# Ten feed-forward tiles of the first MLP go through the down product as seven block products

## The chip, the cores and the metric

The kernel runs on one core of one Trainium2 chip. The metric is the device time of one execution in microseconds (us). Its engines work side by side, each in its own program order, and wait for one another by semaphores: TensorE (PE, matrix products), VectorE (DVE), ScalarE (ACT), GpSimd (POOL), and SyncE (SP), which here issues DMA transfers.

## The reference

A trunk of two pre-norm layers over 512 tokens of width 1024: layer 0 has grouped-query and latent attention, layer 1 neighbourhood attention. After each attention stands the same kind of MLP, and the end is an RMSNorm. All is float32.

```python
def rmsnorm(x, g):
    return x * lax.rsqrt(jnp.mean(x * x, axis=-1, keepdims=True) + EPS) * g

def sq_relu_mlp(h, w_up, w_down):          # w_up 1024 x 4096, w_down 4096 x 1024
    u = jax.nn.relu(h @ w_up)
    return (u * u) @ w_down

# in each of the two layers:
x = x + attention(rmsnorm(x, g_attn))
x = x + sq_relu_mlp(rmsnorm(x, g_ffn), w_up, w_down)
```

## The kernel before

**Number format.** A float32 matrix is kept as two parts of PE's reduced format fp32r: `hi`, a rounded copy made by ACT, and `lo`, the rest, made by DVE as a subtraction. A product is three matmuls, hi by hi, hi by lo and lo by hi. Weights arrive by DMA as `raw`, and become `whi` (ACT L212, or L306 for block products) and `wlo` (DVE L202, L307). They are loaded five chunks ahead of their use, and converted two ahead.

**Slots.** Thirty slots of [128, 1024] float32 hold what lives through the MLP: the normalised tokens, the hidden tiles `U` and raw weight chunks where a slot is free (otherwise one of four `raw` buffers).

**Plain product.** `product` takes for each of four output tiles (four PSUM banks) and for each tile of the summed dimension three matmuls of 512 columns (L496, L497, L498).

**Seven block products.** Class `Seven` takes two output tiles and two k-tiles (a k-pair) as a 2 x 2 block matrix, and the 512 tokens as two halves of 256, and forms the product from seven block products instead of eight. For that it needs sums and differences of blocks on both sides. On the weights' side `seven_chunk` loads 256 KB and makes three subtractions on POOL (L300, L301, L302) for each k-pair. On the token side `sums` makes three subtractions on POOL (L335 to L337), and `split` makes hi (ACT L358) and lo (DVE L359). `run` is then 21 matmuls of 256 columns for each k-pair (L383, L384, L385), and the end of a pair of tiles puts the seven results together: one copy on ACT (L391) and four additions on DVE (L392 to L395).

**The MLP.** The hidden width of 4096 is 32 tiles, taken in four stages of 6, 10, 8 and 8 tiles (`SIZES`). A stage makes its hidden tiles by the up product (relu and square on ACT, L1131 and L1132, and hi and lo, ACT L822 and DVE L819), and then adds their down product to the residual stream `hT` (DVE L1223). The first six tiles are plain (`plain`): there the tokens aren't normalised yet, and each result is scaled by the tokens' `rb` (DVE L1116, ACT L1118). The other 26 come in 13 pairs by `Seven` from normalised tokens `x7`, over four k-pairs (1024 / 256). All down products are plain: a stage of n tiles is 8 output tiles by n k-tiles by 3 matmuls, so 24 n matmuls of 512 columns. While the first down product runs, `later` is called after each of its steps, and issues at the steps (0, 2), (0, 10), (0, 18) and (1, 4) a whole split of one k-pair of x7 (four hi and four lo) at once.

**What sets the order.** The program is written as generators. A scheduler puts the instructions of each engine in an order of its own, by estimated costs; a yielded number is the estimate for a step of PE. `tc.keep_in_program_order` pins an instruction to the place on its engine where the code wrote it.

**After the MLP.** Behind the first MLP stands layer 1's value projection `valuesC`, which takes hT times the norm's weights (ACT L502, DVE L503) as its tokens, and the sum of squares `acc` (ACT L510, DVE L512) for the norm, which PE adds up over the partitions at L517. The last MLP ends the program, with a function of its own; its down product has the lines L1565 to L1567, and the transposes L1579 to token order, which ACT copies at L1580.

Of the kernel before, what the change touches and what calls it, by code (L numbers as in the profile page):

```python
# [16 lines left out]
S = 512  # L17
D = 1024
P = 128
# [16 lines left out]
def encoder_kernel(ctx: ExitStack, tc: tile.TileContext, ins, out, dbg=None):  # L36
# [253 lines left out]

    SEVEN = [(0, 0), (2, 2), (4, 5), (3, 3), (5, 4), (6, 1), (1, 6)]

    def seven_chunk(w, k0, c0):


        slot = Slot(F32) if len(free) > 1 else None
# [3 lines left out]
        POOL.tensor_tensor(r[:, 6], r[:, 0], r[:, 1], op=ALU.subtract)  # L300
        POOL.tensor_tensor(r[:, 4:6], r[:, 2:3].to_broadcast([P, 2, P]), r[:, 0:7:6], op=ALU.add)  # L301
        POOL.tensor_tensor(r[:, 7], r[:, 3], r[:, 5], op=ALU.subtract)  # L302
        yield
        hi = wp.tile([P, 1024], F32R, tag="whi", name=nm("whi"))
        lo = wp.tile([P, 1024], F32R, tag="wlo", name=nm("wlo"))
        ACT.activation(hi[:, 0:896], raw[:, 128:1024], AF.Copy)  # L306
        DVE.tensor_tensor(lo[:, 0:896], raw[:, 128:1024], f32(hi[:, 0:896]), op=ALU.subtract)  # L307
        if slot:
            slot.free()
        yield hi, lo, []  # L310

    class Seven:
# [6 lines left out]
            self.np = nk // 2  # L319

        def number(self, kp, b):
            return 3 * kp + b if b < 3 else 3 * self.np + 4 * kp + b - 3
# [6 lines left out]
        def sums(self, kp, fill_x):  # L329
            raw, t = Slot(F32), Slot(F32)  # L330
# [5 lines left out]
            POOL.tensor_tensor(t_[:, 2], r[:, 2], t_[:, 0], op=ALU.subtract)  # L336
            POOL.tensor_tensor(t_[:, 3], r[:, 3], t_[:, 2], op=ALU.subtract)  # L337

        def split(self, kp):
            for b in range(7):  # L340
                i = self.number(kp, b) // 2
                if i not in self.slots:
                    self.slots[i] = Slot()
            raw, t = self.raw.pop(kp)
            r, t_ = (s_.t.rearrange("p (b n) -> p b n", n=256) for s_ in (raw, t))
            b = 0
            while b < 7:
                q = self.number(kp, b)
                n = 2 if b in (3, 5) or (b < 2 and q % 2 == 0) else 1
                s_ = r[:, 1 + b : 1 + b + n] if b < 3 else t_[:, b - 3 : b - 3 + n]  # L350
                if n == 1:
# [7 lines left out]
                DVE.tensor_tensor(lo, s_, f32(hi), op=ALU.subtract)  # L359
                b += n  # L360
            raw.free()
            t.free()

# [1 line left out]
            for s_ in self.slots.values():  # L365
                s_.free()

        def plan(self, w, c0):
            return [plan(w, 2 * kp, c0, make=seven_chunk) for kp in range(self.np)]

        def run(self, ids, evac):

            bk = group(4)
            half = lambda b, z: b[:, 256 * z : 256 * z + 256]

            dst = [(bk[0], 0), (bk[1], 0), (bk[1], 1), (bk[2], 0), (bk[2], 1), (bk[3], 0), (bk[3], 1)]
            for kp in range(self.np):
                hi, lo = weights(ids[kp])
                for (a, b), (bank_, z) in zip(SEVEN, dst):
                    x = self.at(kp, b)  # L380
                    wh, wl = (y[:, P * a : P * a + P] for y in (hi, lo))
                    o = half(bank_, z)
                    PE.matmul(o, wh, x[:, 0], start=kp == 0 and z == 0, stop=False, skip_group_check=True)  # L383
                    PE.matmul(o, wh, x[:, 1], start=False, stop=False, skip_group_check=True)  # L384
# [6 lines left out]
            ACT.activation(r[:, 3], half(bk[0], 0), AF.Copy)  # L391
            DVE.tensor_tensor(r[:, 1:3], r[:, 3:4].to_broadcast([P, 2, 256]), two(bk[1]), op=ALU.add)  # L392
            DVE.tensor_tensor(r[:, 0:4:3], r[:, 2:3].to_broadcast([P, 2, 256]), two(bk[2]), op=ALU.add)
            DVE.tensor_tensor(r[:, 2], r[:, 3], half(bk[2], 0), op=ALU.add)
            DVE.tensor_tensor(r[:, 0:4:3], r[:, 0:4:3], two(bk[3]), op=ALU.add)  # L395
            evac(w_)
            w_.free()

    flip = [0]

# [693 lines left out]

    SIZES = (6, 10, 8, 8)

    def first_product(l):

# [7 lines left out]
        U = []  # L1108
        rb = keep([P, S], F32, "rb")
        state = dict(c=SIZES[0], ids=None, plain=False)  # L1110
        x7 = Seven(KD)

        def ev(j, b):
# [13 lines left out]
        def fill_x(k, dst):  # L1127
            DVE.scalar_tensor_tensor(dst, hT[:, k, :], gffn(l, k), rb, op0=ALU.mult, op1=ALU.mult)

        def pair_evac(w_):  # L1130
            ACT.activation(w_.t, w_.t, AF.Relu)  # L1131
            ACT.activation(w_.t, w_.t, AF.Square)  # L1132
            first, second = Slot(), Slot()
            split(w_.t[:, S:], first.pair())
            split(w_.t[:, 0:S], second.pair())
            U.extend((first, second))

        def plain():
            four = product(w, 0, xp, tiles(0, 512), ev, lambda n: [mmb(), mmb(), mmb(), sbk()])
            two = product(w, 0, xp, tiles(512, 256), ev, lambda n: [sbk(), ob()], kstep=4)  # L1140
            for n, _ in enumerate(four):
                if n == (11 if l == 0 else 13):
                    norm()
                if n == 14:
                    x7.sums(0, fill_x)
                    x7.sums(1, fill_x)
            for n, _ in enumerate(two):
                if n == 4:
                    x7.sums(2, fill_x)
                if n == 6:  # L1150
                    x7.sums(3, fill_x)
# [12 lines left out]

        def stage(n):
            if not state["plain"]:
                plain()
            while len(U) < n:
                i = state["ids"]
                state["c"] += 2  # L1170
                if len(U) + 2 < n:
                    ahead()
                for _ in x7.run(i, pair_evac):
                    pass
            if state["c"] == 32:
                x7.free()
            got = list(U)
            U.clear()
            return got

        return stage, ahead, later
# [4 lines left out]
    def bias_rows():  # L1186
# [24 lines left out]
            s_.free()  # L1211
        yield

    def mlp(l):
        stage, ahead, later = first_product(l)
        bias = bias_rows()
        k0 = 0
        for z, n in enumerate(SIZES):
            U = stage(n)
            up = [s_.pair() for s_ in U]  # L1220

            def ev(m, b):
                DVE.tensor_tensor(hT[:, m, :], hT[:, m, :], b, op=ALU.add)  # L1223

            gens = [product(ins["ffn_w_down"][l], k0, up, tiles(512 * c, 512), lambda j, b, c=c: ev(4 * c + j, b))
                    for c in range(2)]
            k0 += n
            if k0 < 32:
                ahead()
            for c, gen in enumerate(gens):  # L1230
                for i, _ in enumerate(gen):
                    if z == 0:
                        later(c, i)
                    elif z == 1:
                        next(bias, None)
            for s_ in U:
                s_.free()

    mlp(0)

# [274 lines left out]
    def last_mlp(l):  # L1515
# [77 lines left out]
            return run  # L1593

        k0 = 0
        for n in SIZES:
            U = stage(n)
            if k0 == 0:
                H.extend(Slot(F32) for _ in range(4))
            last = k0 + n == 32  # L1600
# [66 lines left out]
```

## Time and profile before

| | |
|---|---|
| three runs, us | 1194.74, 1194.07, 1195.89 (median 1194.74) |
| the profiled execution, us | 1197.61 |
| its span, us | 1195.8 |
| mean granted PE clock | 0.997 |
| busy: PE, DVE, ACT, POOL, us | 1175.3, 797.0, 614.4, 421.1 |
| first MLP, down product of ten tiles | 386.53 to 442.49 |
| first MLP, last down product | 566.50 to 611.17 |

The span runs from the first to the last instruction; the execution's time holds 1.8 us more around it. PE is busy in 98% of the span, so the time is nearly that of PE's own instructions, and the places where PE waits are few.

### The profile page before, as it was taken

The numbers are of one execution on the slowest core, as the hardware profiler recorded it, in microseconds if no ns is written. First come the engines' busy times: TensorE is split into PE (matmuls) and PEld (weight loads), VectorE is DVE, ScalarE is ACT, GpSimd is POOL, SyncE is SP. The second block draws the span as 40 slices with busy tenths as digits, with TensorE's granted clock in tenths as the row PEclk, the third lists the DMA queues.
The fourth block names the chain that finished last, engine by engine and source line by source line (L and its number), as shares of the span: only waits on it lengthen the run. The fifth ranks groups of instructions, "written<-read, shape, count | busy, mean of one in ns | idle before, by whom it ended". The sixth has DMA issues, their size and how long they took to land.

```text
span 1195.8 us, 18740 instructions
## 1 busy us (share of the span) xinstructions
PE 1175.3 (98%) x6804; PEld 1010.0 (84%) x6804; DVE 797.0 (67%) x1411; ACT 614.4 (51%) x1037; POOL 421.1 (35%) x551
## 2 busy tenths in 40 slices
PE   9999999999999999999999999999999999999997
PEld 8677788887799889889888998988879988988985
DVE  4588988877867437547554676667984743664754
ACT  5577677764447226427433555545463641551653
POOL 3256252216564175341002232231454525434500
PEclk9999999999999999999999999999999999999999
DMA  7223314222522752430336574343342233333122
GB/s 253 64 56 91 86 53 133 71 62 80 176 70 69 228 178 71 133 98 27 105 88 176 129 180 128 114 113 98 115 132 79 63 123 97 98 116 115 54 89 71
DMA packets 105244, 127.96 MB, mean 107 GB/s; under 512 B 8787, under 2 KB 77312, under 8 KB 105152
## 3 DMA queue, kind: packets, MB, share of 16 engines
q1 hardware_dynamic: 102096, 119.30, 33.4%
q0 software_dynamic: 2304, 6.31, 2.2%
q10 hardware_dynamic: 752, 1.15, 0.4%
q8 instruction: 54, 0.88, 0.3%
q14 instruction: 38, 0.31, 0.1%
HBM read 104.32 MB, written 6.29 MB: 92 GB/s over the span
## 4 chain that ended last, share of the span: by engine, by line
PE 83%; DVE 7%; ACT 4%; POOL 3%; issue 2%; DMA 1%; POOLq 0%; DVEq 0%; ACTq 0%
PE mm L497 7%; PE mm L496 7%; PE mm L498 7%; PE mm L385 2%; PE mm L384 2%; PE mm L383 2%; PE s L986 2%; PE o L974 2%; PE s L496 2%; PE s L497 2%; PE s L498 2%; PE mm L1566 2%; PE mm L1565 2%; PE mm L1567 2%; PE t L961 2%
## 5 line engine op out<-in xcount | busy, mean ns | idle before, releaser
L202 DVE TENSOR_TENSOR wlo<-raw,whi 128x1024 fp32r<-128x1024 f32 (+2 forms) x135 | 159.7, 1186 | 142.4 <-ACT whi L212 131.4
L212 ACT ACTIVATE whi<-raw 128x1024 fp32r<-128x1024 f32 (+2 forms) x138 | 135.2, 981 | 167.8 <-PE o L497 38.0
L496 PE MATMUL mm<-a,whi 128*128 128x512 f32 x455 | 184.1, 406 | 0.2 <-DVE hT L920 0.2
L307 DVE TENSOR_TENSOR wlo<-a,whi 128x896 fp32r<-128x896 f32 x99 | 116.0, 1172 | 100.3 <-ACT whi L306 99.6
L497 PE MATMUL mm<-a,whi 128*128 128x512 f32 x455 | 181.0, 398 | 1.1 <-DVE a L819 1.0
L498 PE MATMUL mm<-a,wlo 128*128 128x512 f32 x455 | 180.7, 398 | 0.7 <-DVE wlo L202 0.7
L306 ACT ACTIVATE whi<-a 128x896 fp32r<-128x896 f32 x99 | 94.1, 951 | 142.4 <-PE o L384 26.9
L300 POOL TENSOR_TENSOR a<-a 128x128 f32<-128x128 f32 x99 | 61.8, 624 | 244.8 <-DMA a<-in_ffn_w_up_dram 207.0
L498 PEld LDWEIGHTS mm<-a,wlo 128*128 128x128 f32 x455 | 85.7, 189 | 22.1 <-issue 1.7
L497 PEld LDWEIGHTS mm<-a,whi 128*128 128x128 f32 x455 | 86.0, 189 | 20.0 <-issue 1.7
L496 PEld LDWEIGHTS mm<-a,whi 128*128 128x128 f32 x455 | 86.0, 189 | 19.1 <-issue 1.9
L301 POOL TENSOR_TENSOR a<-a 128x256 f32<-128x256 f32 x99 | 86.2, 871 | 7.8
L302 POOL TENSOR_TENSOR a<-a 128x128 f32<-128x128 f32 x99 | 80.3, 811 | 7.8
L385 PE MATMUL mm<-a,wlo 128*128 128x256 f32 x280 | 78.7, 281 | 0.7 <-DVE wlo L307 0.6
L384 PE MATMUL mm<-a,whi 128*128 128x256 f32 x280 | 78.6, 281 | 0.0
L383 PE MATMUL mm<-a,whi 128*128 128x256 f32 x280 | 78.5, 280 | 0.0
L994 POOL TENSOR_SCALAR p<-p,ti 128x512 f32<-128x512 f32 x64 | 46.0, 720 | 88.5 <-DVE ti L993 74.5
L1368 POOL TENSOR_SCALAR p<-p,ti 128x256 f32<-128x256 f32 x64 | 35.9, 571 | 105.5 <-DVE ti L1367 92.3
L384 PE MATMUL t<-a,whi 128*128 128x256 f32 x192 | 53.9, 281 | 0.0
L385 PE MATMUL t<-a,wlo 128*128 128x256 f32 x192 | 53.8, 280 | 0.0
L383 PE MATMUL t<-a,whi 128*128 128x256 f32 x192 | 53.8, 280 | 0.0
L385 PEld LDWEIGHTS mm<-a,wlo 128*128 128x128 f32 x280 | 52.7, 188 | 1.1 <-DVE wlo L307 1.1
(321 smaller groups left out, 3217.3 us busy)
## 6 DMA issues: line engine op xcount, KB each, us to landing
raw<-in_ffn_w_down_dram SPq DMA_DIRECT2D x64, 512.0 KB
a<-in_ffn_w_up_dram SPq DMA_DIRECT2D x99, 256.0 KB
raw<-in_od_w_qkv_dram SPq DMA_DIRECT2D x64, 128.0 KB
raw<-in_ffn_w_up_dram SPq DMA_DIRECT2D x12, 512.0 KB
raw<-in_ev_w_in_dram SPq DMA_DIRECT2D x12, 384.0 KB
a<-a SPq DMA_DIRECT2D x18, 256.0 KB
bias<-bx SPq DMA_DIRECT2D x16, 256.0 KB
raw<-in_od_w_qkv_dram SPq DMA_DIRECT2D x8, 512.0 KB
```

The lines of the kernel that those rows point to most:

```text
L202: z = lambda: (eng or DVE).tensor_tensor(to, src, f32(high), op=ALU.subtract)
L212: ACT.activation(hi[:, 0:m], raw[:, 0:m], AF.Copy)
L301: POOL.tensor_tensor(r[:, 4:6], r[:, 2:3].to_broadcast([P, 2, P]), r[:, 0:7:6], op=ALU.add)
L302: POOL.tensor_tensor(r[:, 7], r[:, 3], r[:, 5], op=ALU.subtract)
L306: ACT.activation(hi[:, 0:896], raw[:, 128:1024], AF.Copy)
L307: DVE.tensor_tensor(lo[:, 0:896], raw[:, 128:1024], f32(hi[:, 0:896]), op=ALU.subtract)
L383: PE.matmul(o, wh, x[:, 0], start=kp == 0 and z == 0, stop=False, skip_group_check=True)
L384: PE.matmul(o, wh, x[:, 1], start=False, stop=False, skip_group_check=True)
L385: PE.matmul(o, wl, x[:, 0], start=False, stop=kp == self.np - 1, skip_group_check=True)
L496: PE.matmul(o, wh, xh, start=first, stop=False)
L497: PE.matmul(o, wh, xl, start=False, stop=False)
L498: PE.matmul(o, wl, xh, start=False, stop=last)
```

## The change

In the first MLP the stages become 6, 8, 8 and 10 tiles, and the last ten go through the down product as seven block products.

- The up products of the third stage and of the last ten tiles run in a row: nine pairs. The last five pairs only get relu and square and stay raw float32 (`R`).
- While the plain down product of the third stage runs, `convert` makes from the raw pairs what block products need: three subtractions for each pair, on DVE (L336, L338, L340), then hi (ACT L362) and lo (DVE L363), one step for each step of PE, with the DVE instructions pinned.
- After it, `u7.run` runs four times, each over five k-pairs and two output tiles, with weight chunks of w_down made by `seven_chunk`; its end adds [128, 1024] to hT at once (DVE L1286). While the order of these loads is planned, seven_chunk takes slots only while more than eight are free (`reserve`).
- In both MLPs the splits of x7 are made in single pinned steps, one for each step of PE, instead of four lumps.
- In `run` the banks are filled in another order, and the end of a pair writes in another order. The last MLP keeps plain down products in its stages 6, 10, 8, 8. The value projection takes its first two banks from two groups, `[ob(), sbk()]`.

PE's order loses 240 matmuls of 512 columns and gains 420 of 256. In the changed kernel the lines are those of the diff's right side (L202 and L212 stay, L306 is L308, L307 is L309, L359 is L363, L819 is L824, L1116 is L1121, L1223 is L1257, L496 to L498 are L501 to L503, L383 to L385 are L388 to L390).

```diff
-            for z in range(2):
-                fill_x(2 * kp + z, raw.t[:, S * z : S * z + S])
...
-            POOL.tensor_tensor(t_[:, 0:2], r[:, 0:1].to_broadcast([P, 2, 256]), r[:, 1:3], op=ALU.subtract)
+            held(eng.tensor_tensor(t_[:, 0:2], r[:, 0:1].to_broadcast([P, 2, 256]), r[:, 1:3], op=ALU.subtract))
+            yield
...
-                DVE.tensor_tensor(lo, s_, f32(hi), op=ALU.subtract)
+                held(DVE.tensor_tensor(lo, s_, f32(hi), op=ALU.subtract))
                 b += n
+                yield
...
-    SIZES = (6, 10, 8, 8)
+    SIZES = (6, 8, 8, 10), (6, 10, 8, 8)
...
+        def raw_evac(w_):
             ACT.activation(w_.t, w_.t, AF.Relu)
             ACT.activation(w_.t, w_.t, AF.Square)
+            R.append(w_)
+            return True
...
+            for _ in state["split"] if (c, n) in ((0, 10), (0, 18), (1, 4)) else ():
+                pass
             if (c, n) in ((0, 2), (0, 10), (0, 18), (1, 4)):
-                x7.split({(0, 2): 0, (0, 10): 1, (0, 18): 2, (1, 4): 3}[c, n])
+                state["split"] = x7.split({(0, 2): 0, (0, 10): 1, (0, 18): 2, (1, 4): 3}[c, n], tc.keep_in_program_order)
+            next(state["split"], None)
...
+    def convert(u7, R):
+        held = tc.keep_in_program_order
+        for kp, raw in enumerate(R):
+            yield from u7.sums(kp, raw, DVE, held)
+            yield
+            yield from u7.split(kp, held)
...
+            raw = SIZES[l][3] if z == 2 else 0
+            U, R = stage(n, raw)
...
-            if k0 < 32:
+            if raw:
+                u7 = Seven(raw)
+                ids = [u7.plan(w, 256 * m, k0) for m in range(4)]
+                reserve[0] = 8
+                work = convert(u7, R)
+            else:
                 ahead()
...
+                    if raw:
+                        next(work, None)
...
+        for m in range(4):
+            def evac(w_):
+                h2 = hT[:, 2 * m : 2 * m + 2, :]
+                DVE.tensor_tensor(h2, h2, w_.t.rearrange("p (z n) -> p z n", z=2), op=ALU.add)
+            for _ in u7.run(ids[m], evac):
+                pass
+        u7.free()
...
-    first = valuesC(0, lambda: [sbk(), sbk()])
+    first = valuesC(0, lambda: [ob(), sbk()])
```

Three places of DVE's order. The first is the start of the first MLP's down product: `sc` with `s_` and `o_` are the last two of the six plain tiles, their `L819` (`L824`) makes lo, and `wlo` are the first down weights. Before:

```order
L1116 SCALAR_TENSOR_TENSOR sc_3298<-s_3245,rb 128x512
L359 TENSOR_TENSOR a_3450<-a_3262,a_3450 128x2x256
L359 TENSOR_TENSOR a_3451<-a_3262,a_3451 128x256
L359 TENSOR_TENSOR a_3452<-a_3263,a_3452 128x2x256
L359 TENSOR_TENSOR a_3453<-a_3263,a_3453 128x2x256
L819 TENSOR_TENSOR a_3297<-sc_3300,a_3297 128x512
L1116 SCALAR_TENSOR_TENSOR sc_3317<-o_3246,rb 128x512
L202 TENSOR_TENSOR wlo_3348<-raw_3331,whi_3347 128x1024
L359 TENSOR_TENSOR a_3451<-a_3275,a_3451 128x256
L819 TENSOR_TENSOR a_3316<-sc_3319,a_3316 128x512
```

After the change:

```order
L1121 SCALAR_TENSOR_TENSOR sc_3298<-s_3245,rb 128x512
L824 TENSOR_TENSOR a_3297<-sc_3300,a_3297 128x512
L1121 SCALAR_TENSOR_TENSOR sc_3317<-o_3246,rb 128x512
L202 TENSOR_TENSOR wlo_3348<-raw_3331,whi_3347 128x1024
L363 TENSOR_TENSOR a_3360<-a_3144,a_3360 128x2x256
L824 TENSOR_TENSOR a_3316<-sc_3319,a_3316 128x512
L363 TENSOR_TENSOR a_3361<-a_3144,a_3361 128x256
```

The lo parts of x7 (L359, now L363) stood between and ahead of the tiles' and the weights' lo; before `wlo_3348` there were twelve of them, and now there is none.

The second is the same place in the last MLP. Before:

```order
L1116 SCALAR_TENSOR_TENSOR sc_9151<-s_9098,rb 128x512
L359 TENSOR_TENSOR a_9334<-a_9116,a_9334 128x2x256
L359 TENSOR_TENSOR a_9395<-a_9128,a_9395 128x2x256
L359 TENSOR_TENSOR a_9396<-a_9129,a_9396 128x2x256
L819 TENSOR_TENSOR a_9150<-sc_9153,a_9150 128x512
L1116 SCALAR_TENSOR_TENSOR sc_9170<-o_9099,rb 128x512
L202 TENSOR_TENSOR wlo_9205<-raw_9188,whi_9204 128x1024
```

After the change:

```order
L1121 SCALAR_TENSOR_TENSOR sc_9527<-s_9474,rb 128x512
L824 TENSOR_TENSOR a_9526<-sc_9529,a_9526 128x512
L1121 SCALAR_TENSOR_TENSOR sc_9546<-o_9475,rb 128x512
L202 TENSOR_TENSOR wlo_9581<-raw_9564,whi_9580 128x1024
L363 TENSOR_TENSOR a_9593<-a_9373,a_9593 128x2x256
```

The splits that stood between the last two tiles now stand behind both.

The third is the end of the first MLP, where the last additions to hT turn into tokens of the value projection (L503, now L508) and the sum of squares (L512, now L517). Before:

```order
L1223 TENSOR_TENSOR hT<-hT,s_6141 128x512
L503 SCALAR_TENSOR_TENSOR a_6256<-hT,gT,a_6256 128x512
L202 TENSOR_TENSOR wlo_6300<-raw_6281,whi_6299 128x1024
L503 SCALAR_TENSOR_TENSOR a_6257<-hT,gT,a_6257 128x512
L512 TENSOR_TENSOR acc_6258<-acc_6258,sc_6325 128x512
L512 TENSOR_TENSOR acc_6258<-acc_6258,sc_6328 128x512
L512 TENSOR_TENSOR acc_6258<-acc_6258,sc_6331 128x512
```

After the change:

```order
L397 TENSOR_TENSOR a_6619<-a_6619,mm_6499 128x2x256
L398 TENSOR_TENSOR a_6619<-a_6619,mm_6500 128x512
L202 TENSOR_TENSOR wlo_6676<-raw_6657,whi_6675 128x1024
L399 TENSOR_TENSOR a_6619<-a_6619,mm_6500 128x256
L400 TENSOR_TENSOR a_6619<-a_6619,s_6501 128x512
L1286 TENSOR_TENSOR hT<-hT,a_6619 128x1024
L508 SCALAR_TENSOR_TENSOR a_6632<-hT,gT,a_6632 128x512
L508 SCALAR_TENSOR_TENSOR a_6633<-hT,gT,a_6633 128x512
L517 TENSOR_TENSOR acc_6634<-acc_6634,sc_6704 128x512
L517 TENSOR_TENSOR acc_6634<-acc_6634,sc_6707 128x512
```

Where four additions of [128, 512] came out of PSUM, the last two tiles are now first put together by four operations, then added at once.

More of the change, by code (lines that the diff above doesn't have):

```diff
@@ L366, in free, with plan @@
                 s_.free()
[L368 to L369 removed]
+        def plan(self, w, c0, k0=0):
+            return [plan(w, k0 + 2 * kp, c0, make=seven_chunk) for kp in range(self.np)]
         def run(self, ids, evac):
@@ L389, in run @@
             two = lambda b: b.rearrange("p (b n) -> p b n", n=256)
[L391 to L397, printed above, removed]
+            ACT.activation(r[:, 1], half(bk[0], 0), AF.Copy)
+            DVE.tensor_tensor(r[:, 0:4:3], r[:, 1:2].to_broadcast([P, 2, 256]), two(bk[1]), op=ALU.add)
+            DVE.tensor_tensor(r[:, 1:3], r[:, 0:1].to_broadcast([P, 2, 256]), two(bk[2]), op=ALU.add)
+            DVE.tensor_tensor(r[:, 0], r[:, 1], half(bk[2], 1), op=ALU.add)
+            DVE.tensor_tensor(r[:, 1:3], r[:, 1:3], two(bk[3]), op=ALU.add)
+            if not evac(w_):
+                w_.free()
     flip = [0]
@@ L1125, in norm, with x_sums, pair_evac @@
             ACT.activation(rb, bk, AF.Copy)
-        def fill_x(k, dst):
-            DVE.scalar_tensor_tensor(dst, hT[:, k, :], gffn(l, k), rb, op0=ALU.mult, op1=ALU.mult)
-        def pair_evac(w_):
+        def x_sums(kp):
+            raw = Slot(F32)
+            for z in range(2):
+                k = 2 * kp + z
+                DVE.scalar_tensor_tensor(raw.t[:, S * z : S * z + S], hT[:, k, :], gffn(l, k), rb, op0=ALU.mult,
+                                         op1=ALU.mult)
+            for _ in x7.sums(kp, raw):
+                pass
+        def raw_evac(w_):
             ACT.activation(w_.t, w_.t, AF.Relu)
             ACT.activation(w_.t, w_.t, AF.Square)
[L1133 to L1136, printed above, removed]
+            R.append(w_)
+            return True
+        def pair_evac(w_):
+            raw_evac(w_)
+            R.pop()
+            for z in range(2):
+                U.append(Slot())
+                split(w_.t[:, S * z : S * z + S], U[-1].pair())
         def plain():
@@ L1595, in last_mlp @@
         k0 = 0
-        for n in SIZES:
-            U = stage(n)
+        for n in SIZES[l]:
+            U, _ = stage(n)
             if k0 == 0:
```

61 lines of the change are left out of this document (35 added, 26 removed).

## The prediction

> **What bounds the kernel now.** I read the page's busy line and its chain first, then the windows of the first MLP's stages, then PE's timeline where it idles, and DVE's and ACT's beside it.
>
> ```profile
> PE 1175.3 (98%) x6804; PEld 1010.0 (84%) x6804; DVE 797.0 (67%) x1411; ACT 614.4 (51%) x1037; POOL 421.1 (35%) x551
> PE 83%; DVE 7%; ACT 4%; POOL 3%; issue 2%; DMA 1%; POOLq 0%; DVEq 0%; ACTq 0%
> 337.00:386.53 49.53, 49.53 (x421) 49.51 (x420) 37.19 (x44) 32.42 (x41) 24.10 (x32) 1.00 0.23 65
> 386.53:442.49 55.96, 55.96 (x242) 45.07 (x241) 21.59 (x25) 13.45 (x14) 24.32 (x35) 1.00 0.67 209
> 442.49:611.20 168.71, 168.71 (x1058) 151.40 (x1057) 101.15 (x121) 80.87 (x101) 47.84 (x60) 1.00 0.30 91
> ```
>
> PE is 98% busy and 83% of the chain, so time is won by fewer PE cycles or by removing one of its few waits. The windows (length, busy time and count of PE, weight loads, DVE, ACT and POOL, then the granted clock, DMA's share and GB/s) are the first MLP's five pairs before its ten-tile product (420 matmuls of 256 columns), that product (240 of 512) and all the rest: PE has no gap in 274 us, at a granted clock of 1.00. What the change does to PE's work there arrives in full, as long as the other engines keep up.
>
> **The product.** Removed: one ten-tile plain down product, 240 matmuls of 512 columns, 55.96 us by its window, 0.233 each. Added: 420 matmuls of 256 columns, exactly what the first window holds: 49.53 us, 0.118 each. The total of tiles elsewhere is the same (6, 8 and 8 plain, 13 pairs up). Difference: 49.53 - 55.96 = **-6.4 us**.
>
> **The splits at the start of the first MLP's down product.** PE's timeline there, then a window of its clock, then DVE's timeline:
>
> ```profile
> 303.83 0.39 PE L496 MATMUL mm<-a,whi 128*128 128x512 f32 x1
> ...
> 311.04 0.40 PE L497 MATMUL mm<-a,whi 128*128 128x512 f32 x1
> 312.17 0.51 PE L498 MATMUL mm<-a,wlo 128*128 128x512 f32 x1 [0.73 <-DVE wlo L202]
> ...
> 313.91 0.51 PE L497 MATMUL mm<-a,whi 128*128 128x512 f32 x1 [1.01 <-DVE a L819]
> ...
> 318.36 0.39 PE L497 MATMUL mm<-a,whi 128*128 128x512 f32 x1
> 315.00:318.00 3.00, 3.00 (x8) 2.34 (x7) 3.00 (x3) 0.00 (x0) 2.84 (x4) 0.50 0.01 2
> 305.58 3.56 DVE L359 TENSOR_TENSOR a<-a,a 128x512 fp32r<-128x512 f32 x4
> 310.21 0.68 DVE L1116 SCALAR_TENSOR_TENSOR sc<-o,rb 128x512 f32<-128x512 f32 x1
> 310.81 1.30 DVE L202 TENSOR_TENSOR wlo<-raw,whi 128x1024 fp32r<-128x1024 f32 x1
> 312.91 0.94 DVE L819 TENSOR_TENSOR a<-sc,a 128x512 fp32r<-128x512 f32 x1
> ```
>
> The last up tile, bank o, is complete before 303.83, since PE is then in the down product. DVE takes it only at 310.21, because x7's lumped lo parts (L359) stand ahead. So PE waits 0.73 us for a weight's lo and 1.01 us for that tile's lo, and runs at a granted 0.50 from 315 to 318. Between the matmuls at 311.04 and 318.36 lie 15, which at 0.233 take 3.50 us; they took 7.32. The excess is 3.8 us. In the new order no L363 stands ahead of these. Without the 3.56 us of four splits alone, the tile's lo ends at 313.85 - 3.56 = 310.3, and PE first wants it about 312. The splits themselves run later, one a step, and x7 is wanted only from 337.0 on, the first window above. I take the whole: **-3.8 us** (bounds: 0 if the tile is late for another reason, -3.8).
>
> What the trace shows first is that 1.74 us of idling, inside some 3 us, went ahead of a half clock. The Trainium skill's page "TensorE: Matmul & The Clock Gate", Part 1, says that the gate goes to half only after a whole idle window of about 3.4 us, which these waits don't fill; by it the dip would have another cause and could stay.
>
> **The same move in the last MLP.**
>
> ```profile
> 881.86 0.40 PE L1567 MATMUL s<-whi,a 128*128 128x512 f32 x1
> 883.68 0.66 PE L1579 MATMUL t<-cst,hT 128*128 128x128 f32 x4 [1.43 <-ACT a L1580]
> 878.25 2.15 DVE L359 TENSOR_TENSOR a<-a,a 128x512 fp32r<-128x512 f32 x3
> 880.92 0.68 DVE L1116 SCALAR_TENSOR_TENSOR sc<-o,rb 128x512 f32<-128x512 f32 x1
> 883.06 0.57 ACT L1580 ACTIVATE a<-t 128x512 f32<-128x512 f32 x1
> ```
>
> The transposes wait for the copy of the ones before, which stands on ACT behind the last tile's L1118, which waits for DVE's L1116, which stands behind three splits of 2.15 us. Start to start 883.68 - 881.86 = 1.82 us instead of 0.23. With the three splits behind it, that L1116 comes at about 878.8, and the copy ends two microseconds earlier, ahead of PE's wish at 882.1: **-1.6 us** (bounds 0 and -1.6).
>
> **The raw pairs' conversion.** Each pair takes on DVE one subtraction of 512 columns and two of 256, and lo of three times 512 and once 256. The nearest rows:
>
> ```profile
> L359 DVE TENSOR_TENSOR a<-a,a 128x512 fp32r<-128x512 f32 x24 | 20.2, 866 | 0.0
> L359 DVE TENSOR_TENSOR a<-a,a 128x256 fp32r<-128x256 f32 x8 | 4.7, 583 | 0.0
> L393 DVE TENSOR_TENSOR a<-a,mm 128x512 f32<-128x512 f32 x14 | 9.6, 687 | 1.5
> L394 DVE TENSOR_TENSOR a<-a,mm 128x256 f32<-128x256 f32 x14 | 5.8, 412 | 0.0
> L202 DVE TENSOR_TENSOR wlo<-raw,whi 128x1024 fp32r<-128x1024 f32 x106 | 133.9, 1265 | 129.0 <-ACT whi L212 118.3 <-DMA raw<-in_od_w_qkv_dram 4.4 <-PE mm L384 2.2
> 482.10:526.80 44.70, 44.70 (x194) 35.99 (x193) 20.22 (x24) 11.40 (x13) 14.93 (x21) 1.00 0.40 130
> ```
>
> So 0.69 + 2 x 0.41 + 3 x 0.87 + 0.58 = 4.7 us a pair, 23.5 us for five. The equal eight-tile stage before (the window) has DVE busy 20.2 of 44.7 us. 20.2 + 23.5 = 43.7 us fit into 44.7, and the fifth pair is wanted only 4 x 2.5 us into the block product. I cost it at nothing; the cover is that stage's length, 44.7 us. The pinned steps come one for each step of PE, some 40 of the stage's 64, so they should end with a third of the stage left. What they hold up on DVE are the weights' lo of that stage, which stand among them in the order, seven in 44.7 us.
>
> **The end.** Now the last two tiles are put together before hT is whole:
>
> ```profile
> 611.85 0.68 DVE L1223 TENSOR_TENSOR hT<-hT,s 128x512 f32<-128x512 f32 x1
> ...
> 614.25 0.74 DVE L503 SCALAR_TENSOR_TENSOR a<-hT,gT,a 128x512 fp32r<-128x512 f32 x1
> 614.91 2.20 DVE L512 TENSOR_TENSOR acc<-acc,sc 128x512 f32<-128x512 f32 x3
> 619.66 0.95 PE L517 MATMUL t<-ones,acc 128*128 128x1 f32 x8
> ```
>
> PE's product ended at 611.2 (the third window). hT was whole 1.3 us later, the last token tile's lo 3.8 us later, acc 5.9 us later, and PE read acc 8.5 us later. After: behind the end stand one weight lo (1.27), L399 and L400 (0.41 + 0.69) and L1286 (1.27, as L202 is as wide): hT is whole near 4.0 us. From hT to the last lo were 2.46 us: the two lo end at 6.4 and 7.1 (0.74 each), and two sums of 0.7 behind them bring acc to 8.4. PE's order has 56 and 59 matmuls of 0.118 us ahead of the two tiles, so 6.6 and 7.0 us, and 72 ahead of acc, 8.5. That is on the edge: **+0.5 us** (bounds 0 and +2, the latter if another weight lo of 1.27 and a sum of 0.7 come in between).
>
> **The sum.** -6.4 - 3.8 - 1.6 + 0.5 = -11.3 us. The profiled execution took 1197.61 us, so 1186.3; the median stands 2.87 us below it (1194.74), which gives **1183.4 us**.
>
> **The rivals.**
>
> *Nothing gained at the starts.* Pinned steps are each a place where DVE waits for ACT's hi, and a waiting DVE holds all behind it; if the tiles' lo come as late as before, only -6.4 + 0.5 is left: 1188.8 us. Against it: in the order no pinned step stands ahead of the last tile.
>
> *A new stall with a half clock.* Where the block product starts or ends, a wait of 1.7 us would again be followed by the excess of 3.8 us seen at 311 us: 1183.4 + 3.8 = 1187.2. The end is the place for it, its bound of +2 is past 1.7.
>
> *The dip stays.* If the half clock at 315 us isn't of the wait, the 3.00 us at 0.50 still lose half their work, 1.5 of the 3.8 us: 1184.9. Against it: no other idle time stands ahead of the dip. The page on the clock gate, above, would have it so.
>
> *POOL becomes the bound, slower.* Now 36 weight chunks for block products follow each other, then 20; PE eats one in 21 x 0.118 = 2.48 us. POOL's rows:
>
> ```profile
> 423.51 0.46 POOL L300 TENSOR_TENSOR a<-a 128x128 f32<-128x128 f32 x1
> ...
> 425.33 0.46 POOL L300 TENSOR_TENSOR a<-a 128x128 f32<-128x128 f32 x1
> 470.24 0.90 POOL L300 TENSOR_TENSOR a<-a 128x128 f32<-128x128 f32 x1
> ...
> 483.69 1.32 POOL L302 TENSOR_TENSOR a<-a 128x128 f32<-128x128 f32 x1
> ```
>
> A chunk takes 425.33 - 423.51 = 1.82 us beside a quiet DVE, but from 470.24 to 485.01 five chunks took 14.8, 2.95 each, in the third window, where DVE is busy for 101 of 169 us: more than PE's 2.48. What saves it is the head start: by the slots, twelve chunks can be made before the stretch begins, so the other 24 have until about 84 us into it (35 x 2.48 less two lo): 3.4 us each. Above that PE waits, and from (84 + 11) / 24 = 4.0 us on the whole gain is gone; at 4.5 us the time would be 1183.4 + 24 x 1.1 = 1210. The Trainium skill, page "SBUF — State Buffer", section "SBUF: two separate sides", says that a DVE operation with two SBUF inputs and a GpSimd operation exclude each other for a whole instruction. The rows agree that they slow each other; waiting each time for one lo of 1.27 us, a chunk would be 1.82 + 3 x 1.27 = 5.6, which no row shows.
>
> *The change does not do what it says.* If the conversion takes 1.5 times its price (35 us), DVE exceeds that stage by 11 us, PE waits for the sums, and the time is as before. The rows of L359 (2.15 for three, 3.56 for four) are 0.72 to 0.89 us each and don't reach there.
>
> **How the numbers follow.** The forecast as summed 0.58 (own range 1181.5 to 1186), the dip stays 0.05, a new stall 0.10, nothing gained at the starts 0.14, no change 0.05, POOL or DVE as the bound 0.08. Within 0.2% (2.4 us, about what a measurement of this kernel can tell) is the fifth case alone; the last is slower; the others, 0.87, are faster. The range: below, all terms with the end at nothing, 1194.74 - 11.8 = 1182.9, less the 1.8 us by which the three runs differ: 1181. Above, the starts' case with the end at +2: 1190.3.
>
> **What would show it.** Right: the new block product takes 49.5 us without a gap; no PE wait and a clock of 1.00 at the first MLP's start; no wait at the last MLP's first transposes; PE's wait for acc at the end below a microsecond. Wrong: PE waiting for DVE's lo in the nine-pair stretch, for L363 behind the third stage, or a PEclk below 0.9 anywhere in the first MLP.

## The result

The changed kernel took 1187.26 us (median of four runs, 1186.68 to 1187.91) against 1195.14 us before; the ratio is 0.9935, with a 95% interval of 0.9918 to 0.9952. In a second timing it was 0.9941 (0.9929 to 0.9953). The forecast was 1183.4 us, within 1181 to 1190.3: the direction holds and the time lies inside the range, but the gain is 7.9 us where 11.3 were forecast. The profiled execution took 1186.68 us, its span is 1184.9.

The page of the changed kernel, first the busy time of each engine, then each engine's share of the chain of work that ended last:

```profile
PE 1167.6 (99%) x6984; PEld 1014.0 (86%) x6984; DVE 836.2 (71%) x1458; ACT 628.4 (53%) x1061; POOL 475.5 (40%) x611
PE 90%; DVE 4%; ACT 2%; POOL 1%; issue 1%; DMA 1%; SPq 0%; DVEq 0%; POOLq 0%; ACTq 0%
```

PE is 7.7 us less busy and its share of the chain rose from 83% to 90%: the waits for DVE and ACT have shrunk. Windows of the changed kernel's stages (length, then busy time and count of PE, weight loads, DVE, ACT, POOL; granted clock; DMA's share and GB/s): nine pairs in a row, the third plain down product, the new block product, and the start of the value projection:

```profile
417.58:507.33 89.75, 89.71 (x758) 89.30 (x756) 68.17 (x76) 57.59 (x73) 62.52 (x77) 1.00 0.24 71
507.33:552.09 44.76, 44.76 (x195) 36.03 (x193) 38.14 (x55) 18.64 (x27) 22.82 (x29) 1.00 0.43 142
552.09:601.74 49.65, 49.65 (x421) 49.65 (x420) 42.89 (x48) 27.05 (x36) 26.86 (x31) 1.00 0.23 67
601.74:614.59 12.85, 12.85 (x110) 12.77 (x109) 10.66 (x26) 4.86 (x7) 0.00 (x0) 1.00 0.55 156
```

The block product takes 49.65 us without a gap (49.53 forecast), for 55.96 us of the plain one. The nine pairs take 89.75 us where 36 x 2.478 are 89.2. At the start of the first down product DVE's timeline now reads:

```profile
302.85 0.68 DVE L1121 SCALAR_TENSOR_TENSOR sc<-o,rb 128x512 f32<-128x512 f32 x1
303.70 1.23 DVE L202 TENSOR_TENSOR wlo<-raw,whi 128x1024 fp32r<-128x1024 f32 x1 [0.18 <-ACT whi L212]
304.85 0.68 DVE L363 TENSOR_TENSOR a<-a,a 128x512 fp32r<-128x512 f32 x1
305.45 0.68 DVE L824 TENSOR_TENSOR a<-sc,a 128x512 fp32r<-128x512 f32 x1
```

The last tile leaves its bank at 302.85 instead of 310.21, its lo is there at 306.1, and PE has no wait in the whole of the down product.

A table of stretches of PE's timeline (starts of its first matmuls), for before, for the changed kernel, and for a further profile of before that the next section comes to (us):

| stretch | before, profiled 1197.61 | before, profiled 1193.77 | changed, 1186.68 | changed, 1188.71 |
|---|---|---|---|---|
| to the first MLP's last plain up tiles | 276.70 | 276.87 | 276.77 | 277.91 |
| from there to the first up pair (the first down product) | 60.31 | 57.05 | 56.48 | 56.52 |
| from there to the value projection's plain part | 287.19 | 287.18 | 281.34 | 281.66 |
| the last MLP's plain up tiles and first down product | 60.49 | 60.51 | 58.77 | 58.77 |
| from there to the end of the span | 284.2 | 283.5 | 284.5 | 285.0 |

The stretch between the third and the fourth row, layer 1's attention, takes 226.9 to 227.0 us in all four.

### The profile page after: what moved, and what is told of

Same layout as the page of the kernel before. It is cut to its first block, busy times and chain, and to the rows that moved or that the text cites. A ratio compares the mean times of both kernels' runs of the same rounds, so it can differ in the third digit from the quotient of the medians.

```text
span 1184.9 us, 19304 instructions
## 1 busy us (share of the span) xinstructions
PE 1167.6 (99%) x6984; PEld 1014.0 (86%) x6984; DVE 836.2 (71%) x1458; ACT 628.4 (53%) x1061; POOL 475.5 (40%) x611
## 4 chain that ended last, share of the span: by engine, by line
PE 90%; DVE 4%; ACT 2%; POOL 1%; issue 1%; DMA 1%; SPq 0%; DVEq 0%; POOLq 0%; ACTq 0%
PE mm L501 7%; PE mm L503 7%; PE mm L502 7%; PE mm L390 3%; PE mm L388 3%; PE mm L389 3%; PE t L388 2%; PE t L389 2%; PE t L390 2%; PE s L501 2%; PE s L503 2%; PE s L502 2%; PE s L991 2%; PE mm L1618 2%; PE mm L1619 2%; PE mm L1620 2%
## 5 line engine op out<-in xcount | busy, mean ns | idle before, releaser
L202 DVE TENSOR_TENSOR wlo<-raw,whi 128x1024 fp32r<-128x1024 f32 (+4 forms) x125 | 149.4, 1198 | 99.5 <-ACT whi L212 93.6
L309 DVE TENSOR_TENSOR wlo<-a,whi 128x896 fp32r<-128x896 f32 x114 | 138.5, 1217 | 85.2 <-ACT whi L308 84.9
L212 ACT ACTIVATE whi<-raw 128x1024 fp32r<-128x1024 f32 (+2 forms) x128 | 124.8, 975 | 119.7 <-PE o L1620 30.6
L308 ACT ACTIVATE whi<-a 128x896 fp32r<-128x896 f32 x114 | 107.9, 949 | 138.3 <-PE s L389 26.0
L501 PE MATMUL mm<-a,whi 128*128 128x512 f32 x425 | 171.7, 406 | 0.2 <-DVE hT L925 0.2
L502 PE MATMUL mm<-a,whi 128*128 128x512 f32 x425 | 168.4, 396 | 0.2 <-DVE a L545 0.2
L503 PE MATMUL mm<-a,wlo 128*128 128x512 f32 x425 | 168.0, 396 | 0.0
L302 POOL TENSOR_TENSOR a<-a 128x128 f32<-128x128 f32 x114 | 71.1, 624 | 192.9 <-DMA a<-in_ffn_w_up_dram 160.5
L303 POOL TENSOR_TENSOR a<-a 128x256 f32<-128x256 f32 x114 | 100.9, 885 | 8.9
L304 POOL TENSOR_TENSOR a<-a 128x128 f32<-128x128 f32 x114 | 100.3, 880 | 8.9
L503 PEld LDWEIGHTS mm<-a,wlo 128*128 128x128 f32 x425 | 79.6, 188 | 19.6 <-issue 1.7
L501 PEld LDWEIGHTS mm<-a,whi 128*128 128x128 f32 x425 | 79.9, 188 | 17.7 <-issue 1.4
L390 PE MATMUL mm<-a,wlo 128*128 128x256 f32 x330 | 92.6, 281 | 0.4 <-DVE wlo L309 0.4
L389 PE MATMUL mm<-a,whi 128*128 128x256 f32 x330 | 92.7, 281 | 0.0
L388 PE MATMUL mm<-a,whi 128*128 128x256 f32 x330 | 92.7, 281 | 0.0
L389 PE MATMUL t<-a,whi 128*128 128x256 f32 x232 | 65.2, 281 | 0.0
L388 PE MATMUL t<-a,whi 128*128 128x256 f32 x232 | 65.1, 280 | 0.0
L390 PE MATMUL t<-a,wlo 128*128 128x256 f32 x232 | 64.9, 280 | 0.0
L390 PEld LDWEIGHTS mm<-a,wlo 128*128 128x128 f32 x330 | 62.1, 188 | 0.8 <-DVE wlo L309 0.8
```

The costliest lines, as they stand in the source:

```text
L202: z = lambda: (eng or DVE).tensor_tensor(to, src, f32(high), op=ALU.subtract)
L212: ACT.activation(hi[:, 0:m], raw[:, 0:m], AF.Copy)
L388: PE.matmul(o, wh, x[:, 0], start=kp == 0 and n in (0, 1, 3, 5), stop=False, skip_group_check=True)
L501: PE.matmul(o, wh, xh, start=first, stop=False)
L502: PE.matmul(o, wh, xl, start=False, stop=False)
L503: PE.matmul(o, wl, xh, start=False, stop=last)
```

## The experiments

### What a single profile of before is worth

The difference between the two profiled executions is 10.9 us, that between the medians 7.9. The kernel before and the changed one were run again, unchanged.

> The kernel before, unchanged, timed against itself. Theory A (the difference of the two profiled executions, 10.9 us, is the change's worth, and 7.9 us between the medians is only run-to-run spread): medians within 1.5 us of each other, single runs spread over 3 us and more. Theory B (the half clock after the first down product's waits comes in some executions only; the profiled one of before had it): the runs fall near 1194 to 1195 where the mean granted clock is 0.998 or 0.999 and 1.5 to 2 us higher where it is 0.997; a new profile shows the two waits of 0.7 and 1.0 us at 312 us again, but a half clock behind them perhaps not.

Against itself before has a ratio of 0.9998 (0.9990 to 1.0007), with runs from 1193.13 to 1197.15 us.

> The changed kernel, unchanged, beside the kernel before on the same chip. Theory A: 8 to 10 us below the median of before, and the profiled difference near 11 us only where the granted clocks differ. Theory B: differences between single runs follow the mean granted clock, some 1.2 us for each 0.001 of it.

The changed kernel: 1188.56 us, runs from 1187.60 to 1188.85, ratio 0.9941. So the changed kernel's runs spread over 1.3 us and before's over 4. Neither theory held as written: the changed kernel is 6.3 us below before's 1194.86 and not 8 to 10, and the mean granted clock orders before's runs badly (1193.68 us at 0.997, 1196.62 at 0.999). Sorted, the 64 timed runs of before in this study can be parted at a small gap (0.34 us wide) into 37 from 1193.1 to 1195.1 and 27 from 1195.4 to 1197.8, and both of its profiles so far were of the upper group. Two more profiles were to show a lower one.

> The kernel before once more, one profile. The 36 runs of it so far fall into groups at 1193.1 to 1194.9 and 1195.4 to 1197.4 us, and both profiles so far (1197.61 and 1197.15) are of the upper one. Theory C (the stall at the first down product's start is there in some executions only: in the lower group PE does not wait at 312 us at all, in the middle it waits, in the upper a half clock follows): if this execution is at or below 1194.9 us, its trace has less than 0.5 us of waits at 312; near 1195.5 the two waits without a half clock; at 1197 both. Theory D (the stall is always there and the spread is elsewhere): the two waits of 0.6 to 1.0 us at every time.

> The same kernel before, a further profile, for the same question: theory C ties the execution's time to what happens at 312 us (no wait: 1193 to 1195; waits: 1195 to 1196.3; waits and half clock: 1196.4 and more), theory D does not.

They took 1193.77 and 1194.24 us. PE's, DVE's and POOL's timelines of the first of them at 305 to 313 us:

```profile
312.36 0.51 PE L497 MATMUL mm<-a,whi 128*128 128x512 f32 x1 [0.32 <-DVE a L819]
305.77 2.22 DVE L359 TENSOR_TENSOR a<-a,a 128x512 fp32r<-128x512 f32 x4
307.91 0.69 DVE L819 TENSOR_TENSOR a<-sc,a 128x512 fp32r<-128x512 f32 x1
305.97 2.95 POOL L300 TENSOR_TENSOR a<-a 128x128 f32<-128x128 f32 x1 [7.37 <-DVE sc L1116]
```

POOL's timeline of before's first profile (1197.61 us), at the same place:

```profile
305.51 0.46 POOL L300 TENSOR_TENSOR a<-a 128x128 f32<-128x128 f32 x1 [7.10 <-DMA a<-in_ffn_w_up_dram]
306.05 1.07 POOL L301 TENSOR_TENSOR a<-a 128x256 f32<-128x256 f32 x1
```

In the upper execution POOL's first subtraction for a weight chunk starts at 305.51, just ahead of DVE's run of four splits (305.58), and the two alternate: the run takes 3.56 us, and PE waits 0.73 and 1.01 us with a half clock behind. In the lower one POOL comes 0.2 us after the run's start, its 0.46 us operation takes 2.95 us, and DVE's run takes 2.22: PE waits 0.32. The other profile of the upper group (1197.15 us) has a run of 3.45 us and waits of 0.63 and 1.01, the other of the lower group (1194.24 us) a run of 2.22 and a wait of 0.28. Theory C holds in these four: whether POOL starts just ahead of the run or just behind its start is worth 3.3 us (60.31 against 57.05 in the table). What decides it is likely the landing of the chunk's transfer, which the profile names as what POOL waited for in three of the four; in the lower execution shown here it names DVE's L1116, so this part is not shown.

To make it happen rather than see it happen, POOL's first eight chunks in before were made to wait for the last plain tile:

```diff
...
+                gate.extend([f32(up[5][:, 1, 0:1])] * 8)
...
+        if gate:
+            POOL.tensor_copy(r[:, 6, 0:1], gate.pop())
         POOL.tensor_tensor(r[:, 6], r[:, 0], r[:, 1], op=ALU.subtract)
```

> The kernel before, with one thing added: the first eight weight chunks' subtractions on POOL must wait until the last plain tile's lo part is made (a copy of one column from it into a place that the subtraction then overwrites). The orders of PE, DVE, ACT and SP stay as they are. In the four profiles of before so far, POOL's first subtraction came in just ahead of DVE's run of four splits twice (the run took 3.56 us, PE waited 1.7 us and a half clock followed), and just behind its start twice (2.22 us, PE waited 0.3). Theory C (who comes first decides): the run takes 2.2 us in the profile, PE waits 0.3 us or not at all at 312, all runs lie at 1193 to 1194.9 and spread under 2 us, median 1 us below before. Rival (the spread of before is elsewhere): runs at 1195.4 to 1197.4 as often as in before.

DVE's, PE's and POOL's timelines of it:

```profile
306.29 2.23 DVE L363 TENSOR_TENSOR a<-a,a 128x512 fp32r<-128x512 f32 x4
311.97 0.40 PE L502 MATMUL mm<-a,wlo 128*128 128x512 f32 x1
311.93 2.84 POOL L303 COPY a<-a 128x1 f32<-128x1 f32 x4 [15.05 <-DVE a L823]
```

The run takes 2.23 us, PE does not wait at all, and the stretch takes 56.51 us, as in the changed kernel. All eleven runs lie from 1193.77 to 1195.03 us; of the fifteen of before beside it, five lie from 1195.57 to 1197.12. So the upper group needs POOL at this place. The gate keeps POOL away altogether, so that the order of arrival decides rests on the four profiles above. The median did not fall by the 1 us expected (1194.63 against 1194.75, ratio 0.9995, 0.9986 to 1.0004): the kernel is the lower group, not faster than it.

### The two parts of the change, each alone

Before, with x7's splits alone in single pinned steps (`split` also gets the `yield` and the pin of the changed kernel):

```diff
...
-                x7.split({(0, 2): 0, (0, 10): 1, (0, 18): 2, (1, 4): 3}[c, n])
+                state["split"] = x7.split({(0, 2): 0, (0, 10): 1, (0, 18): 2, (1, 4): 3}[c, n], tc.keep_in_program_order)
+            next(state["split"], None)
```

> The kernel before with one part of the change alone: x7's splits in both MLPs as single pinned steps, one for each step of PE, instead of four lumps. If the prediction's terms hold: no wait at the first down product's start (-3.8 us in the trace if the half clock goes with it) and none at the last MLP's first transposes (-1.6): 5.4 us below the kernel before's profiled execution, 3.5 to 5.4 below its median. Rival (the pins move the waits elsewhere): within 1 us of the kernel before. If the half clock at 315 us has another cause, -2.3 and -1.6: 3.9.

1192.43 us (1191.85 to 1193.22), ratio 0.9979 (0.9970 to 0.9988): 2.4 us, less than the 3.5 to 5.4 expected. In the trace all waits that were to go are gone: the stretch of the first down product takes 56.50 us and the last MLP's 58.84. From the upper execution of before that is 3.8 and 1.65 us, 5.5 together; from the lower one 0.5 and 1.65, so 2.2, near the 2.4 of the medians.

The changed kernel with the splits in lumps again:

```diff
...
-                state["split"] = x7.split({(0, 2): 0, (0, 10): 1, (0, 18): 2, (1, 4): 3}[c, n], tc.keep_in_program_order)
-            next(state["split"], None)
+                for _ in x7.split({(0, 2): 0, (0, 10): 1, (0, 18): 2, (1, 4): 3}[c, n]):
+                    pass
```

> The changed kernel with x7's splits in four lumps and not pinned, as before; the block products of the last ten tiles stay. If the terms add: only the product's -6.4 us is left (less 0.7 us for two short waits in the nine-pair stretch), so 5.5 to 6.5 us below the kernel before and 3.5 to 5.4 above the changed one, and the waits of 0.7, 1.0 and 1.4 us are back in the trace. Rival (the change's gain comes mostly from the splits): within 2 us of the kernel before.

1190.04 us, ratio 0.9961 (0.9947 to 0.9975): 4.8 us below before (5.5 to 6.5 were expected), 1.5 above the changed kernel (3.5 to 5.4). Its five runs are again in two groups, 1189.48 to 1190.04 and 1191.74 to 1192.38. The profile is of the upper one. PE's timeline, then a window of the clock:

```profile
313.02 0.51 PE L503 MATMUL mm<-a,wlo 128*128 128x512 f32 x1 [0.55 <-DVE wlo L202]
...
314.76 0.50 PE L502 MATMUL mm<-a,whi 128*128 128x512 f32 x1 [1.01 <-DVE a L824]
316.00:318.00 2.00, 2.00 (x10) 1.63 (x9) 2.00 (x3) 0.00 (x0) 1.84 (x4) 1.00 0.00 0
```

Here the waits came (58.58 us for the stretch, 2.1 above 56.5) and no half clock followed. In both upper profiles of before it did, and they took 1.6 and 1.7 us more. The two parts add, in medians: 2.4 for the splits and 4.8 for the product are 7.2; the whole gave 6.3 beside them and 7.9 before.

### The covers that the prediction relied on

Conversion. Every DVE instruction of it issued twice:

```diff
...
-                held(DVE.tensor_tensor(lo, s_, f32(hi), op=ALU.subtract))
+                for _ in range(1 + twice[0]):
+                    held(DVE.tensor_tensor(lo, s_, f32(hi), op=ALU.subtract))
```

and the three subtractions in the same way.

> The changed kernel with every DVE instruction of the raw pairs' conversion issued twice (the second writes the same values): 35 more, 21.7 us more of DVE by the changed kernel's trace, where the conversion ended at 540 us, 12 us ahead of the block product. If the stage covers the conversion as the prediction has it: conversion ends near 562, the fifth pair is wanted at 562, so 0 to 5 us slower than the changed kernel, by a wait for L363 or a weight's lo at the block product's start. Rival (the conversion is on the path already): 15 to 22 us slower.

1203.45 us, 14.9 above the changed kernel, ratio to before 1.0065 (1.0049 to 1.0080). PE's timeline, DVE's, and windows of it:

```profile
554.72 0.58 PE L394 MATMUL o<-a,whi 128*128 128x256 f32 x1 [8.10 <-DVE hT L1265]
553.99 0.68 DVE L1265 TENSOR_TENSOR hT<-hT,o 128x512 f32<-128x512 f32 x1
548.00:552.00 4.00, 0.00 (x0) 0.00 (x0) 4.00 (x7) 1.26 (x2) 1.87 (x3) 0.56 0.00 0
556.00:560.00 4.00, 3.54 (x8) 2.81 (x9) 4.00 (x7) 0.00 (x0) 3.65 (x1) 0.50 0.47 142
```

Close to the rival's number, by a way that no theory had. The wait is not for the pairs, but for the addition of a finished plain bank to hT (L1265), which stands behind the conversion on DVE, so that the bank isn't free. PE waits 8.1 us for it and then runs at 0.50 until about 562. The scheduler had also moved some block matmuls ahead of the last plain ones, one of which needs that bank; what the doubled work would have cost in the old order was not tried. By the sum of the work alone DVE had 38.1 + 21.7 = 59.8 us to do in a stage of 44.8, 15.1 too many, and that is nearly what it cost.

The conversion unpinned:

```diff
...
-            yield from u7.sums(kp, raw, DVE, held)
+            yield from u7.sums(kp, raw, DVE)
             yield
-            yield from u7.split(kp, held)
+            yield from u7.split(kp)
```

> The changed kernel with the raw pairs' conversion not pinned on DVE: the scheduler places its 35 instructions. If the pins only keep an order that would come anyway: within 1 us of the changed kernel. If unpinned conversion slips behind the weights' lo and comes late: PE waits at the block product's start, 1 to 6 us slower. If the pins hold up the weights' lo: up to 1 us faster.

1187.25 us (1186.57 to 1187.99), ratio 0.9929 (0.9916 to 0.9943). The changed kernel has 1187.26 and 1188.56 in its two timings: no difference that can be told. The pins aren't what makes the conversion work.

POOL. One of the three subtractions for a weight chunk issued twice, or three times, in the first MLP:

```diff
...
-        POOL.tensor_tensor(r[:, 4:6], r[:, 2:3].to_broadcast([P, 2, P]), r[:, 0:7:6], op=ALU.add)
+        for _ in range(1 + heavy[0]):
+            POOL.tensor_tensor(r[:, 4:6], r[:, 2:3].to_broadcast([P, 2, P]), r[:, 0:7:6], op=ALU.add)
```

> The changed kernel with the second of POOL's three subtractions for a weight chunk issued twice (the same values again), in the first MLP alone. In the changed kernel's nine-pair stretch eight chunks in a row take 2.77 us each on POOL, so about 3.6 here. By the prediction's limit of 3.4 us for a chunk: 24 x 0.2 = 5 us slower than the changed kernel; if POOL's idle time there (14.5 us of 90) is free to use: 0 to 1 us slower; if POOL sets the pace already: 20 us slower.

> The same with that subtraction issued three times, about 4.5 us for a chunk. By the prediction's limit of 3.4: 24 x 1.1 = 26 us slower than the changed kernel. If POOL isn't what paces the stretch at all: within 2 us of it.

1214.47 us (1214.24 to 1215.25) and 1260.23 us (1258.80 to 1260.72): 26 and 72 us above the changed kernel, ratios to before 1.0158 (1.0144 to 1.0172) and 1.0537 (1.0523 to 1.0552). Windows of the nine pairs and of the block product with the value projection's first part, with one more subtraction, and then PE's longest waits (us in total, times, the longest):

```profile
418.86:522.14 103.28, 95.68 (x757) 93.67 (x756) 69.11 (x76) 55.95 (x70) 92.33 (x109) 0.95 0.21 62
567.65:630.05 62.40, 55.41 (x432) 54.05 (x431) 45.94 (x48) 27.81 (x37) 45.35 (x54) 0.95 0.18 52
PE s L391 <- ACT whi L311: 7.5, 3, 3.9
PE mm L393 <- DVE wlo L312: 3.5, 7, 0.8
PE s L393 <- DVE wlo L312: 3.2, 5, 1.0
```

In the first window POOL makes 27 chunks of the 36, one every 3.65 us, and is busy for 92.3 of 103.3 us. The limit is near where the prediction had it: 27 chunks in 89.2 us are 3.3 us each, and 3.65 is over it. What was too low was the price: 13.5 us instead of 5, since PE idles 7.6 us (103.28 less 95.68) and pays a half clock behind its waits. And a second stretch, the block product, has a limit of this kind too: alone it ran from 567.65 to 628.76, 61.1 us, so it lost 11.5, where the prediction looked for nothing. With two more subtractions the two stretches lost 44 and 22 us.

### A further step the same way

```diff
...
-    SIZES = (6, 8, 8, 10), (6, 10, 8, 8)
+    SIZES = (6, 8, 6, 12), (6, 10, 8, 8)
```

> The changed kernel with stages of 6, 8, 6 and 12 tiles in the first MLP: twelve tiles go through the down product as block products. Product's arithmetic: 48 matmuls of 512 columns fewer and 84 of 256 more, 1.3 us less than the changed kernel. Cover: six pairs take 26 us of DVE in a third stage of 33.6 us, beside some 13 us of other DVE work, so the conversion runs 5 us over, but the sixth pair is wanted 12 us into the block product. If the cover holds: 1.3 us below the changed kernel. Rival: the shorter stage leaves waits of 1 to 5 us, no gain or a loss of up to 4 us.

1188.79 us (1188.31 to 1190.53), ratio 0.9945 (0.9933 to 0.9958): level with the changed kernel. A window of its third down product, and PE's waits for a weight's lo in block products over the whole program (one of the four, 0.6 us, is in the last MLP):

```profile
507.80:541.29 33.49, 33.49 (x146) 27.04 (x145) 33.32 (x52) 16.96 (x24) 15.19 (x16) 1.00 0.29 94
PE s L390 <- DVE wlo L309: 1.6, 2, 1.3
PE mm L390 <- DVE wlo L309: 1.4, 2, 0.7
```

PE has 1.3 us less to do and waits for the weights' lo instead: DVE is busy in 33.3 of the shorter stage's 33.5 us, and the longest wait, 1.3 us, stands at 547.9, 6.6 us behind that stage. No version run here beats the changed kernel clearly.

## Why the prediction was right, and 3.9 us too low

**The product, -6.4.** The block product itself is right to 0.1 us. The stretch that holds it gave 5.8 and 5.5 us in the two profiles (287.2 to 281.3 and 281.7): 0.6 to 0.9 came back in the nine pairs, where PE waits for a weight's lo in the middle, and the end gave 0.2. PE waiting for DVE's lo there was on the prediction's own list of signs of being wrong; it came, but small (the longest wait is 0.3 us). After that the last MLP's rest takes 0.8 us more, 284.6 as a mean of the eight profiles of kernels with the change's `run` (284.2 to 285.2) against 283.8 of the six without it (283.5 to 284.3). The two ranges touch, so this is a tendency; what does it wasn't tried and is open. With it the sum comes near the 4.8 us that the product alone gave.

**The first down product's start, -3.8.** Right for the execution that was profiled (60.31 to 56.48), wrong for the kernel: in the two lower profiles of before the stall was about 0.5 us, and 37 of 64 runs have times like theirs. The step took one profile's stall for every run's.

**The last MLP, -1.6.** It was 1.7, in upper and lower executions alike. PE's timeline of the changed kernel has the transposes without a wait:

```profile
869.40 0.60 PE L1632 MATMUL t<-cst,hT 128*128 128x128 f32 x4
```

**The end, +0.5.** It was -0.2: 13.04 us before, 12.85 after. DVE's timeline of the changed kernel:

```profile
605.27 1.22 DVE L1286 TENSOR_TENSOR hT<-hT,a 128x1024 f32<-128x1024 f32 x1
607.29 1.41 DVE L508 SCALAR_TENSOR_TENSOR a<-hT,gT,a 128x512 fp32r<-128x512 f32 x2 [0.79 <-ACT a L507]
608.62 1.48 DVE L517 TENSOR_TENSOR acc<-acc,sc 128x512 f32<-128x512 f32 x2
```

From the product's end at 601.74, hT is whole at 4.75 us (4.0 forecast), the last lo is there at 7.0 (7.1) and acc at 8.4 (8.4). The chain was right, and PE's wish of 7.0 and 8.5 was met on the edge, so nothing was lost.

**The conversion, 0.** DVE's groups in the third plain product of the changed kernel (busy us, mean ns of one, idle time before them):

```profile
L363 DVE TENSOR_TENSOR a<-a,a 128x512 fp32r<-128x512 f32 x15 | 10.5, 734 | 0.0
L336 DVE TENSOR_TENSOR a<-a 128x512 f32<-128x512 f32 x5 | 3.9, 778 | 0.0
L363 DVE TENSOR_TENSOR a<-a,a 128x256 fp32r<-128x256 f32 x5 | 2.6, 524 | 0.0
L340 DVE TENSOR_TENSOR a<-a,a 128x256 f32<-128x256 f32 x5 | 2.4, 473 | 0.1
L338 DVE TENSOR_TENSOR a<-a,a 128x256 f32<-128x256 f32 x5 | 2.3, 463 | 0.0
```

Together 21.7 us (23.5 forecast), done at 540.0, 12 us ahead of the block product. Hidden, as forecast.

**The step that failed** is the last of the sum, with the size of the stall in it. -11.3 us from the profiled 1197.61 gives 1186.3, and the changed kernel's profiled execution took 1186.68. Then the prediction took off another 2.87 us, since before's median stood that far below its profiled execution. But that distance was for the most part the stall itself: the lower executions, to which the median run of 1194.74 us belongs by its time, have 0.5 us of it and not 3.8 (57.05 and 60.31 in the table). The sum had already counted it as gained, so it was counted twice. From a lower execution (1193.8 us) with -5.5, -0.5, -1.7 and +0.8 the sum is 1186.9.

**The rivals.** "A new stall with a half clock" is nearest in time (1187.2), and by chance: it did not come, since in the changed kernel's two profiles every 1 us window from 250 to 610 us has a clock of 1.00. "Nothing gained at the starts" (1188.8) is near the second timing, but its mechanism isn't there: no pinned step holds up a tile. "The dip stays": the half clock goes with the wait, but doesn't follow it every time. POOL as the bound did not come, at 2.77 us a chunk (eight from 453.14 to 475.31) for a limit of 3.3; the two runs with more work on POOL show how near that edge is.

## What to carry to other kernels

Before a stall in a profile is counted as a gain, ask whether the other runs have it: a profiled execution that is slower than the median may be slower by that very stall, and then the distance must not be taken off a second time. A cover is measured by doubling what it hides. The price beyond its edge can be more than the overflow, as with POOL (27 chunks 0.35 us over the limit are 9.5 us, and the stretch lost 13.5), since a wait of PE can draw a half clock behind it; and it can come at another place than expected, as where work queued on DVE held up a bank that PE needed next. Where two engines slow each other, a fraction of a microsecond in which of them starts first can decide a kernel's group of times; single steps instead of lumps took that spread away as well as the wait.

## What the runs showed of the hardware

DVE and POOL do not share evenly: who starts first keeps the other out. A POOL subtraction that takes 0.46 us alone took 2.95 us when it began 0.2 us into DVE's run of four splits, and that run then took its undisturbed 2.22 us; when POOL came first, the same four took 3.56 us. In the first case POOL was kept out by five DVE instructions in a row, the four splits and the L819 behind them, which ended at 308.60; POOL's operation ended at 308.92. The Trainium skill, page "SBUF — State Buffer", section "SBUF: two separate sides", has DVE operations with two SBUF inputs and GpSimd operations exclude each other, whichever starts first; the traces agree, in both orders, and show that work that follows without a gap can keep the other engine out for longer than one instruction.

The half clock after PE's idling is not certain: 1.74 and 1.64 us of waits within 3 us were followed by 0.50 in two profiles of before, and 1.56 us were not in the changed kernel with lumps. A wait of 8.1 us (the conversion issued twice) was followed by it. The Trainium skill's page "TensorE: Matmul & The Clock Gate", Part 1, has a window of about 3.4 us that runs freely, and a half clock behind a whole idle one. A free window that happens to lie over the waits or not would fit the first two cases, but the waits there fill only half of one, so a whole idle window is more than these runs asked for.
